# HGRN scores as needed 128x32 blocks with levels in pairs, and fp32 transposes as two 64-row tiles

## The chip, the cores and the metric

The kernel runs on one core of a Trainium2 chip. The metric is the device time of one execution in microseconds (us); the median of several runs is compared. In the profile PE is TensorE's matmuls, PEld its weight loads, DVE VectorE, ACT ScalarE, POOL GpSimd, SP the engine that issues most DMAs.

## The reference, cut to what matters

One layer for a prompt of 512 frames and a sample of 32: two branches, mLSTM (4 heads of 512) and HGRN2 (8 heads of 128), merged by sigmoid gates, then an output projection. The change concerns the HGRN2 branch, and wherever a tile is transposed.

```python
def _hgrn_chunk(S, inp):
    q, k, v, lf = inp
    g = jnp.cumsum(lf, axis=2)
    dec = jnp.exp(jnp.where(causal, g[:, :, :, None, :] - g[:, :, None, :, :], -jnp.inf))
    a = jnp.einsum('bhtc,bhtsc,bhsc->bhts', q, dec, k)
    o = jnp.einsum('bhtc,bhce->bhte', q * jnp.exp(g), S) + jnp.einsum('bhts,bhse->bhte', a, v)
    ...
```

The decay `dec` differs by channel, so the scores `a` are no plain product of q and k.

## The kernel before, in words

Activations stand transposed, channels on the 128 partitions and the 544 frames (32 of the sample, 512 of the prompt) in the columns. All dense products run in float32r, split into a high and a low part, three matmuls each; many projections are formed as pairs (`Two`) by a Strassen-like scheme, whose matmuls write the PSUM tiles named `d` (L608). TensorE's order is written by hand: a `Pump` holds the stream of `d` matmuls, six to a step, and the special work of a head is a generator (`mchain` for an mLSTM head, `chain` for an HGRN head) that yields the number of steps to run before its next piece. The order on VectorE and ScalarE comes from the framework's scheduler, by priorities and its own estimate of times. Small products use two PSUM tiles of two banks in turn (`paux`).

`chain(h)` computes an HGRN head. The scores of a block of 128 keys and 128 queries are made by levels: at level c = 1, 2, 4 ... 64, queries and keys that lie in neighbouring groups of c meet with the decay up to the border between them. At each level ScalarE copies the keys in a swapped order into `km` (L1818), TensorE multiplies them with the queries `qq`, for both blocks, 128x128 in fp32 (two passes each, L1832), VectorE copies what that level contributes into `at` by a mask (L1857), and multiplies the decay of the level into `kk` and `qq`, which lie in one tile `hkq` (L1850). Level 16 also makes the sample's scores out of copies (`snap`) that were taken at the four levels before (L1823, L1834, L1836, L1861). So of each 128x128 product only the blocks next to the diagonal at that level are used.

The rest of a head: `pd` transposes q times k for the diagonal (L1871), `ht` turns values and keys (L1902, L1903), `su` makes the states (L1921), `ho` the outputs from the triangles `aa` of `at`, which POOL cuts (L1797, L1945 to L1949); VectorE normalises them (L1951 to L1967), and `finish` of the head before, inside the next head's chain, turns them back (`hoT`, L1975, L1976) and multiplies by gain and gate (L1979, L1980). In `mchain`, `kt`, `kts`, `vt`, `vts` turn keys and values of an mLSTM head (L1122, L1135, L1157, L1175), and `yt` its outputs (L1307, L1308). All of these transposes are fp32 matmuls of 128 rows against the identity; a transpose is one pass.

Of the kernel before, what the change touches and what calls it, by code (L numbers as in the profile page):

```python
# [9 lines left out]
F32 = mybir.dt.float32  # L10
# [7 lines left out]
P = 128  # L18
# [18 lines left out]
QUADS = P // NS  # L37
STEPS = (2, 3, 3, 3, 3, 3, 3)
# [29 lines left out]
def hybrid_step(ctx: ExitStack, tc: tile.TileContext, a, o):  # L68
# [45 lines left out]
    def psplit(src, name, ring):  # L114
        hi, lo = pair_tile(name, ring)
        S.copy(hi, src)
        V.tensor_tensor(lo, src, hi.bitcast(F32), ALU.subtract)
        return hi, lo

# [196 lines left out]
    def masks():  # L316

        t = cp.tile([P, T], F32, tag="lm", name="lmask")
        u, n = t[:, :T].bitcast(U8), len(LEVELS) * HB
        return u[:, :n].rearrange("p (l t) -> p l t", l=len(LEVELS)), u[:, n : n + NS]  # L320
# [791 lines left out]
    def mchain(h, pump):  # L1112
# [5 lines left out]
        for b in range(NB):  # L1118
            yield 4 if h else 1
            pt = paux(f"kt{h}{b}")  # L1120
            for f in range(KH):
                PE.transpose(pt[:, 0, f * P : (f + 1) * P], kf[f][:, NS + b * P : NS + (b + 1) * P], ident)  # L1122
            kh, kl = slot(f"kwh{h}{b}", F32R), slot(f"kwl{h}{b}", F32R)
            wc = col[:, 10 + b, h : h + 1]
            with tc.high_priority():
                kh_ = S.mul(kh[:, :HD], pt[:, 0, :], wc)
                kl_ = V.scalar_tensor_tensor(kl[:, :HD], pt[:, 0, :], wc, kh[:, :HD].bitcast(F32), ALU.mult, ALU.subtract)
# [4 lines left out]
        yield 4 if h else 2  # L1132
        pt = paux(f"kts{h}")
        for f in range(KH):
            PE.transpose(pt[: 3 * NS, 0, f * P : (f + 1) * P], ksm[:, f], ident)  # L1135

        kws = small("kws", [3 * NS, HD], F32R, bufs=1)
        wc = cols[:, 1, h : h + 1]
        with tc.high_priority():
            S.mul(kws, pt[: 3 * NS, 0, :], wc)  # L1140
            lo = slice(2 * NS, 3 * NS)
            low = V.scalar_tensor_tensor(kws[lo], pt[lo, 0, :], wc[lo], kws[lo].bitcast(F32), ALU.mult, ALU.subtract)
# [6 lines left out]
        else:  # L1149
            yield max(0, max(pump.when["v", f] for f in range(KH)) - pump.done)  # L1150
            vt = t["vt"]
            vv = []
            for b in range(NB):
                yield 1
                pt = paux(f"vt{h}{b}")
                for f in range(KH):
                    PE.transpose(pt[:, 0, f * P : (f + 1) * P], vt[f][:, NS + b * P : NS + (b + 1) * P], ident)  # L1157
# [5 lines left out]
                with tc.high_priority():  # L1163
                    S.copy(vh[:, :HD], pt[:, 0, :])
                    V.tensor_tensor(vl[:, :HD], pt[:, 0, :], vh[:, :HD].bitcast(F32), ALU.subtract)
# [3 lines left out]
            yield 1  # L1169
            pt = paux(f"vts{h}")  # L1170
            vsm, copied = triple(vt, "vsm", t["copied"])
            with tc.issue_after(filled.ins):
                make_late(3 if h < MH - 1 else 2, copied)
            for f in range(KH):
                PE.transpose(pt[: 3 * NS, 0, f * P : (f + 1) * P], vsm[:, f], ident)  # L1175
            vs = small("vs", [3 * NS, VW], F32R, bufs=1)
            with tc.high_priority():
                S.copy(vs[:, :HD], pt[: 3 * NS, 0, :])
            G.tensor_copy(vs[:, HD:VW], vone)
            lo = slice(NS, 2 * NS)  # L1180
            with tc.high_priority():
                low = V.tensor_tensor(vs[lo, :HD], pt[lo, 0, :], vs[lo, :HD].bitcast(F32), ALU.subtract)
# [116 lines left out]
        for f in range(KH):  # L1299
# [3 lines left out]
            yield max(GAP - (16 if h == MH - 1 else 0 if h else 4) if f == 0 else 1 if h else 2, pump.when["z", f] - pump.done)  # L1303
            ft = h * KH + f
            pt = paux(f"yt{ft}")
            for b in range(NB):
                PE.transpose(pt[:, 0, b * P : (b + 1) * P], yb[b][:, f * P : (f + 1) * P], ident)  # L1307
            PE.transpose(pt[:, 1, :P], yb[NB][:, f * P : (f + 1) * P], ident)  # L1308
# [4 lines left out]
            with tc.high_priority():  # L1313
                V.scalar_tensor_tensor(c[:, NS:T], pt[:, 0, :], g, c[:, NS:T], ALU.mult, ALU.add)
                V.scalar_tensor_tensor(c[:, :NS], pt[:, 1, :NS], g, c[:, :NS], ALU.mult, ALU.add)
            with nullcontext() if 0 < h < MH - 1 else tc.high_priority():
# [978 lines left out]
```

## Time and profile before

| | |
|---|---|
| median of 3 runs | 1103.38 us (1103.07 to 1103.73) |
| span of the profiled execution | 1101.5 us, from the first to the last instruction |
| around the span, to the median of the runs | 1.9 us |
| mean granted TensorE clock | 0.998 |
| busy: PE, DVE, ACT, POOL | 99%, 84%, 63%, 19% |
| the eight HGRN heads | 627 to 862 us of the span |

A row of a group reads: line, engine, operation, out<-in, partitions x elements, count | busy us, mean ns of one | idle of the engine before them and what ended it. Of a matmul, 128*32 are rows and columns of the weight tile. A row of a timeline reads: start, length, instruction, count. Of two rows that overlap on PE, the distance of the starts is what the first one costs.

### The profile page before, as it was taken

The page shows a single profiled execution, that of the slowest core. Times are in us where ns is not written, and L with a number is a line of the kernel's source. Part 1 is how long each engine was busy: PE and PEld are TensorE (multiplying, and loading weights), DVE is VectorE, ACT ScalarE, POOL GpSimd, SP SyncE. Part 2 cuts the span into 40 slices and gives each one's busy share as a digit, 9 for nine tenths or more (in the row PEclk, how much of TensorE's full clock was granted, in tenths as well). Part 3 has the DMA queues.
Part 4 walks back from the last instruction along what each step waited for, and adds up shares of the span by engine and source line. Part 5 has one row for each costly group of instructions (what it writes and reads, how often), then busy time and mean ns, then how long its engine had stood idle before and what let it go on. Part 6 is the DMA issues. An engine that isn't in the chain of part 4 may idle for free.

```text
span 1101.5 us, 23773 instructions
## 1 busy us (share of the span) xinstructions
PE 1092.4 (99%) x8625; PEld 1070.9 (97%) x8625; DVE 922.8 (84%) x2103; ACT 693.1 (63%) x1579; POOL 209.5 (19%) x375
## 2 busy tenths in 40 slices
PE   9999999999999999999999999999999999999997
PEld 9899999999999999999999999999999999999997
DVE  7889988686896786986888799999999977778885
ACT  7777557754666554665656476776776666446683
POOL 5204010303022021202120123232232210000002
PEclk9999999999999999999999999999999999999999
DMA  7135415639355276554798665666765683337753
GB/s 241 50 124 157 156 58 185 158 125 220 119 178 179 93 178 176 164 167 146 212 261 254 172 145 141 144 135 152 159 145 150 155 222 103 110 90 242 247 180 121
DMA packets 97262, 176.58 MB, mean 160 GB/s; under 512 B 11284, under 2 KB 18580, under 8 KB 96888
## 3 DMA queue, kind: packets, MB, share of 16 engines
q1 hardware_dynamic: 81072, 141.01, 39.9%
q0 software_dynamic: 15184, 32.93, 16.2%
q8 instruction: 68, 1.11, 0.4%
q10 hardware_dynamic: 888, 1.12, 0.3%
q14 instruction: 50, 0.41, 0.1%
HBM read 150.10 MB, written 41.69 MB: 174 GB/s over the span
## 4 chain that ended last, share of the span: by engine, by line
PE 93%; DMA 3%; DVE 2%; issue 1%; SPq 0%; ACT 0%; POOL 0%; ACTq 0%; POOLq 0%
PE d L608 44%; PE ya L167 9%; PE yb L167 4%; PE q L167 4%; PE k L167 4%; PE C L1077 4%; PE nm L1257 3%; PE sc L1037 2%; PE pl L1832 2%; PE u L291 2%; PE d L460 2%; PE vp L1576 2%; DMA ws<-in_w_in 1%; PE ple L167 1%; PE kt L1122 1%; PE ht L1902 1%
## 5 line engine op out<-in xcount | busy, mean ns | idle before, releaser
L495 POOL DMA_DIRECT2D ws<-in_w_in x46 | 40.2, 875 | 211.3 <-DVE hkq L1850 32.2
L622 ACT COPY t<-d 128x272 f32<-128x272 f32 x153 | 58.0, 379 | 14.0 <-PE d L608 14.0
L1850 DVE TENSOR_TENSOR hkq<-hkq,q 128x288 f32<-128x288 f32 (+1 forms) x96 | 40.7, 431 | 2.6 <-PE pl L1834 1.0
L785 DVE SCALAR_TENSOR_TENSOR cv<-ub,vec,cv 128x547 f32<-128x547 f32 x48 | 37.6, 784 | 1.6 <-ACT cv L780 1.2
L1832 PE MATMUL pl<-hkq,km 128*128 128x128 f32 x224 | 36.2, 283 | 0.6 <-ACT km L1818 0.5
L1818 ACT COPY km<-hkq 128x256 f32<-128x256 f32 x56 | 23.9, 428 | 14.2 <-DVE hkq L1850 5.2
L1832 PEld LDWEIGHTS pl<-hkq,km 128*128 128x128 f32 x224 | 30.3, 189 | 2.0 <-ACT km L1818 1.5
L1191 DVE SCALAR_TENSOR_TENSOR c<-c,wi,Cs 128x258 f32<-128x258 f32 x32 | 15.3, 479 | 18.8 <-PE Cs L1189 18.5
L1354 DVE TENSOR_TENSOR y<-ya,y 128x272 f32<-128x272 f32 x48 | 18.9, 435 | 12.1 <-PE ya L167 10.3
L1089 ACT COPY Co<-C 128x258 f32<-128x258 f32 x30 | 9.8, 378 | 27.3 <-PE C L1077 24.9
L1857 DVE COPY_PREDICATED at<-lmask,pl 128x256 f32<-128x256 uint8 (+1 forms) x56 | 25.2, 451 | 0.1
L777 POOL COPY uo<-ub 128x3 f32<-128x3 f32 x16 | 18.7, 1167 | 34.5 <-DVE ub L631 26.6
L1268 ACT COPY y<-nm 128x516 f32<-128x516 f32 x16 | 9.4, 590 | 23.0 <-PE nm L1257 22.5
L133 POOL TENSOR_TENSOR wple50l<-wple5r,wple50h 128x256 fp32r<-128x256 f32 x1 | 0.7, 736 | 120.9 <-ACT wple50h L132 120.9
L961 POOL COPY ksm<-kf 128x96 f32<-128x96 f32 x16 | 7.1, 445 | 84.9 <-ACT kf L975 84.9
L961 POOL COPY vsm<-vt 128x96 f32<-128x96 f32 x12 | 6.3, 525 | 85.9 <-ACT vt L633 43.5
L1797 POOL TENSOR_SCALAR_AFFINE_SELECT aa<-at 128x128 f32<-128x128 f32 x32 | 19.6, 643 | 8.2 <-DVE at L1857 8.0
L581 POOL DMA_DIRECT2D ws<-in_w_in x14 | 14.6, 1043 | 33.1 <-DVE ws272l L133 27.3
L1245 DVE BATCH_NORM_STATS2 bs<-y 128x6 f32<-128x512 f32 (+1 forms) x20 | 13.8, 692 | 8.3 <-ACT y L1268 8.0
L1257 PE MATMUL nm<-vhl,sh 128*128 128x258 f32 x112 | 18.4, 286 | 0.0
L376 POOL DMA_DIRECT2D w_pg_d<-in_w_pg x16 | 13.1, 818 | 25.1 <-issue 21.4
L1956 ACT ACTIVATE osq<-kq 128x128 f32<-128x128 f32 x32 | 9.8, 305 | 12.4 <-DVE kq L1951 12.1
(4735 smaller groups left out, 5086.7 us busy)
## 6 DMA issues: line engine op xcount, KB each, us to landing
ws<-in_w_in POOLq DMA_DIRECT2D x60, 256.0 KB, 4.9
ws<-in_w_in SPq DMA_DIRECT2D x46, 256.0 KB, 3.9
ya_d<-y SPq DMA_DIRECT2D x32, 272.0 KB, 2.3
y<-ya_d SPq DMA_DIRECT2D x24, 272.0 KB, 3.3
w_out_d<-in_w_out POOLq DMA_DIRECT2D x24, 256.0 KB, 6.5
w_pg_d<-in_w_pg POOLq DMA_DIRECT2D x24, 256.0 KB, 6.5
c<-in_C SPq DMA_DIRECT2D x16, 258.0 KB, 3.8
out_Cs<-c SPq DMA_DIRECT2D x16, 258.0 KB, 3.8
```

The costliest lines, as they stand in the source:

```text
L167: PE.matmul(both[b][:m, :TH], part(w, off + k * step, m, x), xx[:, half(b)], start=(k == 0 and j == 0), stop=(k == n - 1 and j == 2),)
L291: PE.matmul(both[b][:m, :TH], part(w, off + k * step, m, x), xx[:, half(b)], start=(k == 0 and j == 0), stop=(k == KD - 1 and j == 2),)
L495: G.dma_start(t, piece(u, i), accum_op=ALU.add)
L608: PE.matmul(ps, ww[:, c], xx, start=(start and k == 0 and j == 0), stop=end, skip_group_check=not start,)
L622: self.kept = S.copy(t, ps)
L785: V.scalar_tensor_tensor(cv[:, :547], ub[:, j : j + 547], vcol(V_CW + 4 * ft + j), cv[:, :547], ALU.mult, ALU.add)
L1077: PE.matmul(pn[g][:, :VH], kw[b][x][:, f * P : (f + 1) * P], vv[b][y][:, g * VH : (g + 1) * VH], start=(b == 0 and j == 0), stop=(b == NB ...
L1257: PE.matmul(pn[:, g, :VH], st[j][x][:, (i - j) * P : (i - j + 1) * P], vv[j][y][:, g * VH : (g + 1) * VH], start=(j == 0 and q == 0), stop ...
L1818: low = S.copy(km.rearrange("p (n j c) -> p n j c", j=2, c=c), view(kk, HB, ((2 * c, NA // (2 * c)), (c - HB, 2), (1, c))),)
L1832: PE.matmul(out, km[:, b * P : (b + 1) * P], view(qq, b * P, dims), start=True, stop=True)
L1850: V.tensor_tensor(x, x, d, ALU.mult)
L1857: V.copy_predicated(at[:, :n], lmask[:, li, :n], pn[:, 0, :n])
```

## The change

It has three parts.

1. The scores are made only where they are used: for each quarter of 32 keys a matmul of 128x32 weights and 32 queries (64 at level 64), whose output goes to the 32 PSUM partitions of that quarter, so that four stand side by side in the array (`scores`). The levels go in pairs (1), (2, 4), (8, 16), (32, 64): of a pair's first level the queries are kept as a copy `oldq` (and the sample's pair `olds`) and the keys in one half of `kms`, and both levels are multiplied at the second. The sample is made with each level below 32 (four equal tiles). `collect` puts the results into a strip `near` of 96 columns by mask, into `far` (level 32) or straight into `at` (level 64), and four copies spread the strips into `at`. The tile `oldq` lies in has the old name `lmask`.
2. A transpose of 128 rows becomes two of 64 rows (`turn`), whose outputs go to two PSUM banks, and all readers of the PSUM tile take them apart by `turned` and `quarters`. Of the sample only the 64 rows that hold it are turned.
3. Two groups of transposes stand back to back, where a group stood alone: `kt` in pairs, `kts` with `vt0`, `vt1` with `vt2`, `vt3` with `vts`, `yt` in pairs, both `ht`, and `hoT` with `pd`, which is moved from level 1 (and `hoT` from behind level 16) to ahead of level 16's block. The gain of the head is multiplied into the gate ahead of time.

```diff
+    def turn(pt, i, src, eye=None):
+        n = src.shape[-1]
+        for r in range(2):
+            k = slice(r * HP, (r + 1) * HP)
+            at_ = ident[k, k] if eye is None else eye[k, P - (r + 1) * HP : P - r * HP]
+            PE.transpose(pt[:n, r, i * HP : (i + 1) * HP], src[k], at_)
...
         for b in range(NB):
-            yield 4 if h else 1
-            pt = paux(f"kt{h}{b}")
-            for f in range(KH):
-                PE.transpose(pt[:, 0, f * P : (f + 1) * P], kf[f][:, NS + b * P : NS + (b + 1) * P], ident)
+            if b % 2 == 0:
+                yield 8 if h else 2
+                pts = [paux(f"kt{h}{b + i}") for i in range(2)]
+                for i in range(2):
+                    for f in range(KH):
+                        turn(pts[i], f, kf[f][:, NS + (b + i) * P : NS + (b + i + 1) * P])
...
+        def scores(pn, i, c, km, snap):
+            for b in range(2):
+                for g in range(QUADS):
+                    key, w = b * P + g * NS, max(c, NS)
+                    out = pn[g * NS : (g + 1) * NS, i, b * w : (b + 1) * w]
...
+                    PE.matmul(out, km[:, key : key + NS], ask, start=True, stop=True)
+            if c < NS:
+                for g in range(QUADS):
+                    PE.matmul(
+                        pn[g * NS : (g + 1) * NS, i, 2 * NS : 3 * NS],
+                        olds[:, 0] if snap else kk[:, csmp],
+                        olds[:, 1] if snap else qq[:, csmp],
+                        start=True,
+                        stop=True,
+                    )
+
+        def collect(ps, li, c):
+            if c < NS:
+                V.copy_predicated(near, lmask[:, li], ps[:, : 3 * NS])
+            elif c == NS:
+                S.copy(far, ps[:, : 2 * NS])
+            else:
+                for g in range(2):
...
+        def turn_both():
+            if h:
+                pt = turn_out(h - 1)
+            pn = paux(f"pd{h}")
+            for b, c_ in enumerate([c_ for c_, _, _ in chunks] + [slice(NA, NA + P)]):
+                turn(pn, b, kq[:, c_])
+            with tc.high_priority():
+                V.tensor_reduce(dg, turned(pn, NB + 1), AX.XY, ALU.add)
+            if h:
+                finish(h - 1, pt)
+
         for li, c in enumerate(LEVELS):
...
+                if first_:
+                    S.copy(
+                        oldq.rearrange("p (n j c) -> p n j c", j=2, c=c),
+                        view(qq, 0, ((2 * c, NA // (2 * c)), (HB + c, 2), (1, c))),
+                    )
+                    if c < NS:
+                        S.copy(olds, hs[h]["pair"][:, :, csmp])
                 low = S.copy(
                     km.rearrange("p (n j c) -> p n j c", j=2, c=c),
                     view(kk, HB, ((2 * c, NA // (2 * c)), (c - HB, 2), (1, c))),
                 )
-                if li < QUADS:
-                    S.copy(snap[:, :, li], hs[h]["pair"][:, :, csmp])
             held.append(low)
-            yield STEPS[li]
...
+            if not first_:
+                n = STEPS[li] + (STEPS[li - 1] if li else 0)
+                if li == 4:
+                    yield n // 2
+                    turn_both()
+                    n -= n // 2
+                yield n
+
+                pn = paux(f"pl{h}{c}")
+                if li:
+                    scores(pn, 0, c // 2, kms[:, 0], True)
+                scores(pn, 1, c, km, False)
...
-                V.copy_predicated(at[:, :n], lmask[:, li, :n], pn[:, 0, :n])
-                if smp:
-                    for i in range(QUADS):
-                        d = slice(i * NS, (i + 1) * NS)
-                        V.copy_predicated(at[d, NA:HB], smask[d], pn[d, 1, d])
+                if not first_:
+                    if li:
+                        collect(pn[:, 0], li - 1, c // 2)
+                    collect(pn[:, 1], li, c)
+            if c == 2 * NS:
+                for g in range(QUADS):
...
+                    S.copy(at[k, :NA].rearrange("p (b q s t) -> p b q s t", b=2, q=2, s=2)[:, :, g // 2], both_)
```

TensorE, head 3, before: around the scores of level 16 (`pl316`); `hkq3` holds queries and keys, `d...` are the dense matmuls between.

```order
L608 MATMUL d521_10311<-xl5_892,ws452h_10542 128x272
L608 MATMUL d521_10311<-xh5_891,ws452l_10543 128x272
L1832 MATMUL pl316_10642<-hkq3_9838,km316_10610 128x128 x2
L1834 MATMUL pl316_10642<-hkq3_9838 128x32
L1836 MATMUL pl316_10642<-snap_10431 128x128
L608 MATMUL d521_10311<-xh6_908,ws452h_10542 128x272
```

The same place after; `lmask_2805` is `oldq` and `olds`, the queries of level 8.

```order
L625 MATMUL d520_10756<-xfl3_1327,wa2252h_10958 128x272
L625 MATMUL d520_10756<-xfh3_1326,wa2252l_10959 128x272
L1891 MATMUL pl316_11112<-lmask_2805,km38_11007 32x32 x8
L1894 MATMUL pl316_11112<-lmask_2805 32x32 x4
L1891 MATMUL pl316_11112<-hkq3_10210,km38_11007 32x32 x8
L1894 MATMUL pl316_11112<-hkq3_10210 32x32 x4
L625 MATMUL d521_10757<-xh4_886,ws452h_11015 128x272
```

Levels 8 and 16 have become one block of 24 small matmuls, with 18 dense ones ahead of it, and 18 more between the transposes and the pair before.

TensorE, head 3, after: `hoT2` (outputs of head 2) and `pd3`, between the blocks `pl34` and `pl316`.

```order
L625 MATMUL d761_11020<-xh5_891,wa1276l_10941 128x272
L129 MATMUL hoT2_11059<-anti_123,kq2_9663 128x64 x4
L129 MATMUL hoT2_11059<-ident_104,kq2_9663 128x64 x4
L2084 MATMUL hoT2_11059<-anti_123,osb_10696 128x64
L129 MATMUL pd3_11069<-ident_104,kq3_10211 128x64 x10
L625 MATMUL d761_11020<-xh6_908,wa1276h_10940 128x272
```

Before, `pd3` stood six dense matmuls behind level 1 and `hoT2` six behind level 16, each alone; both are now one block.

VectorE, head 3, before: the scaling of head 2's outputs (`kq2`, `osb`), on which `hoT2` waits.

```order
L1850 TENSOR_TENSOR hkq3_9838<-hkq3_9838,q03_10188 128x2x16x8
L185 SCALAR_TENSOR_TENSOR hr_10406<-rsq_u_10415,hr_10406 128x5
L133 TENSOR_TENSOR ws276l_10586<-ws176_10337,ws276h_10585 128x512
L1961 TENSOR_TENSOR kq2_9365<-kq2_9365,hr_10406 128x512
L1967 TENSOR_SCALAR osb_10288<-osb_10288,hr_10406 128x128
L133 TENSOR_TENSOR ws376l_10633<-ws376_10340,ws376h_10632 128x512
L1850 TENSOR_TENSOR hkq3_9838<-hkq3_9838,q03_10188 128x2x9x16
```

And after.

```order
L1904 COPY_PREDICATED at3_10866<-lmask_2805,pl34_10977 128x96
L202 SCALAR_TENSOR_TENSOR hr_10830<-rsq_u_10839,hr_10830 128x5
L200 TENSOR_TENSOR rsq_u_10839<-hr_10830 128x5
L201 SCALAR_TENSOR_TENSOR rsq_u_10839<-rsq_u_10839,hv_10829 128x5
L202 SCALAR_TENSOR_TENSOR hr_10830<-rsq_u_10839,hr_10830 128x5
L2070 TENSOR_TENSOR kq2_9663<-kq2_9663,hr_10830 128x512
L1970 TENSOR_TENSOR hkq3_10210<-hkq3_10210,q03_10619 128x2x18x8
L2076 TENSOR_SCALAR osb_10696<-osb_10696,hr_10830 128x128
L1970 TENSOR_TENSOR hkq3_10210<-hkq3_10210,q03_10619 128x2x16x8
```

The scaling now stands between the masked copy of level 4 and the update of level 8; before it stood behind the update of level 8.

265 lines of the change are left out of this document (155 added, 110 removed).

## The prediction

> **What bounds the kernel.** I read the engines' shares and the chain that ended last, then the stretch of the eight HGRN heads by windows, then the groups of the instructions that the change replaces.
>
> ```profile
> PE 1092.4 (99%) x8625; PEld 1070.9 (97%) x8625; DVE 922.8 (84%) x2103; ACT 693.1 (63%) x1579; POOL 209.5 (19%) x375
> PE 93%; DMA 3%; DVE 2%; issue 1%; SPq 0%; ACT 0%; POOL 0%; ACTq 0%; POOLq 0%
> 627.00:862.00 235.00, 234.36 (x1901) 231.68 (x1899) 227.66 (x631) 167.48 (x464) 65.59 (x94) 1.00 0.64 147
> L1832 PE MATMUL pl<-hkq,km 128*128 128x128 f32 x224 | 36.2, 283 | 0.6 <-ACT km L1818 0.5
> L1871 PE MATMUL pd<-ident,kq 128*128 128x128 f32 x40 | 5.7, 272 | 0.0
> L1122 PE MATMUL kt<-ident,kf 128*128 128x128 f32 x64 | 9.7, 274 | 0.0
> L1307 PE MATMUL yt<-ident,y 128*128 128x128 f32 x64 | 10.0, 273 | 0.2 <-DVE y L1296 0.2
> ```
>
> TensorE carries 93% of the chain, at a clock of 1.00 in the stretch. Its matmuls there wait 0.6 us for `km` and for next to nothing else, so a microsecond taken from TensorE is one from the time, as long as nothing else becomes late. In the heads' stretch VectorE is nearly full too (227.66 of 235), ScalarE is not (167.48). The `x224` are records of passes: an fp32 matmul has two, 112 matmuls being 224; a transpose has one.
>
> A record's length (0.28 us) overlaps the next; what an instruction costs is the distance of starts. So I price a block from the start of the dense matmul before it to that of the second dense matmul behind it, less two dense paces.
>
> ```profile
> 627.62 0.29 PE L608 MATMUL d<-xh,ws472l 128*128 128x272 f32 x1
> 627.75 0.64 PE L1832 MATMUL pl<-hkq,km 128*128 128x128 f32 x4
> 628.13 0.38 PE L608 MATMUL d<-xfh,ws249h 128*128 128x272 f32 x1
> 628.35 0.29 PE L608 MATMUL d<-xfl,ws249h 128*128 128x272 f32 x1
> 628.47 0.29 PE L608 MATMUL d<-xfh,ws249l 128*128 128x272 f32 x1
> 628.85 0.29 PE L608 MATMUL d<-xfh,ws249l 128*128 128x272 f32 x1
> 628.98 0.71 PE L1871 MATMUL pd<-ident,kq 128*128 128x128 f32 x5
> 629.65 0.29 PE L608 MATMUL d<-xfl,ws249h 128*128 128x272 f32 x1
> 670.59 0.29 PE L608 MATMUL d<-xh,ws450l 128*128 128x272 f32 x1
> 670.72 0.61 PE L1832 MATMUL pl<-hkq,km 128*128 128x128 f32 x4
> 671.31 0.47 PE L1836 MATMUL pl<-snap 128*128 128x128 f32 x2
> 671.74 0.29 PE L608 MATMUL d<-xl,ws450h 128*128 128x272 f32 x1
> ```
>
> The dense pace is 0.125 us (628.35 to 628.47, and from 628.47 three more to 628.85). A level of scores costs 628.35 - 627.62 - 0.25 = 0.48 us; level 16, with the sample's extra products, 671.74 - 670.59 - 0.25 = 0.90. A head has six of the one and one of the other, 3.78 us; eight heads 30.2. Five transposes cost 629.65 - 628.85 - 0.25 = 0.55, 0.11 each. The change retiles 380 of them (by the program's order kt 64, kts 16, vt 48, vts 12, yt 80, pd 40, ht 80, hoT 40): 41.8 us. So 72 us of TensorE are in play.
>
> **Scores in 128x32 tiles.** The kernel already has such tiles once, in the sample's values:
>
> ```profile
> 46.56 0.63 PE L1576 MATMUL vp<-wv3h,x 128*128 128x512 f32 x2
> 47.03 0.40 PE L1576 MATMUL vp<-wv3l,x 128*128 128x512 f32 x1
> 47.36 0.62 PE L1586 MATMUL vq<-wv0r,xg 128*32 128x512 f32 x1
> 47.38 0.62 PE L1586 MATMUL vq<-wv3r,xg 128*32 128x512 f32 x1
> 47.81 0.59 PE L1586 MATMUL vq<-wv0r,xg 128*32 128x512 f32 x1
> 47.83 0.59 PE L1586 MATMUL vq<-wv3r,xg 128*32 128x512 f32 x1
> 48.35 0.72 PE L1576 MATMUL vp<-wv4h,x 128*128 128x512 f32 x2
> 48.91 0.40 PE L1576 MATMUL vp<-wv4l,x 128*128 128x512 f32 x1
> ```
>
> Four tiles start within 0.02 us and run side by side; the second pass follows 0.45 later, of which 0.03 is the first weight load (0.62 against 0.59): 0.42 for 512 columns, 0.83 ns each. The dense pace is 0.235 (46.56 to 47.03 is two), so the block costs 48.91 - 47.03 - 3 x 0.235 = 1.18, and entering and leaving the tiling 1.18 - 2 x 0.42 = 0.34.
>
> After the change a level below 32 has three rounds of four tiles (two blocks of keys, one of the sample) of 32 columns in two passes: six passes in a row per tile; level 32 four, level 64 four of 64 columns. That is 34 short passes and 4 long ones a head. A short pass takes at least its load, 0.03, its columns being 0.027. At most it takes the issue of four loads and four matmuls: four starts in 0.02 are 7 ns each, eight are 0.055. I take 0.04, nearer to the streamed row, and for a long pass 0.065, between its columns (0.053) and 0.08: 1.62 us a head (1.24 to 2.2). Levels in pairs give four tilings a head instead of eight or seven.
>
> The Trainium skill, "TensorEngine Tiling (Array Packing)", Instruction Overhead, says that a matmul of one column lasts as long as one of 60, and warns against taking the tiling from a dimension that is already small; no run here shows it for tiles. By it a short pass would be 60 x 0.83 = 0.05 us, an estimate, and the scores would save 2.7 us less than I sum.
>
> **Transposes as two 64-row tiles.** No two row tiles run in the trace. The nearest are transposes of 4-row tiles, which all stand in one row group:
>
> ```profile
> 90.73 0.42 PE L167 MATMUL q<-cs3h,wq001l 128*128 128x272 f32 x2
> 91.08 1.27 PE L916 MATMUL cols<-ident,row 4*128 4x4 f32 x18
> 92.22 0.28 PE L918 MATMUL cols<-ident,r 4*96 4x4 f32 x3
> 92.43 0.52 PE L167 MATMUL q<-cs0h,wq010h 128*128 128x272 f32 x2
> 92.78 0.29 PE L167 MATMUL q<-cs0l,wq010h 128*128 128x272 f32 x1
> ```
>
> They move four columns only and still take (92.22 - 91.08) / 18 = 0.063 us: that is the weight load of 128 columns; with 96 columns 0.05. The second dense matmul started at 90.86, so the block costs 92.78 - 90.86 - 3 x 0.125 = 1.55, and entering and leaving 1.55 - 18 x 0.063 - 3 x 0.05 = 0.27. I take 0.30 for each change of tiling, between this and 0.34.
>
> A transpose becomes two loads of 128 columns and two matmuls of 64 columns (0.053 each). If the two row tiles work side by side, the pair is bound by one load, 0.063; by the columns alone it would be 0.053; if the loads go one after the other, 0.126, more than the 0.11 of now. I take 0.063, as the column tiles did run side by side. The order has 46 blocks of them (four of these are splinters of `yt12`, cut by dense matmuls): 380 x 0.063 + 46 x 0.30 = 37.7 us against 41.8. So it saves 4.1 us; 2.2 with 0.34 a change, 9.2 with 0.053 and 0.27. The change of tiling eats most of it: a block of eight saves 0.88 - 0.50 - 0.30 = 0.08 us, the lone `kts0` loses 0.11.
>
> The scores: 8 x (1.62 + 4 x 0.30) = 22.6 against 30.2, 7.6 saved; with the ends 1.8 to 11.6.
>
> **The other engines.** These rows tell what is taken from VectorE and how the one chain that is pulled forward stands:
>
> ```profile
> L1857 DVE COPY_PREDICATED at<-lmask,pl 128x256 f32<-128x256 uint8 x48 | 21.4, 446 | 0.1
> L1861 DVE COPY_PREDICATED at<-lmask,pl 32x32 f32<-32x32 uint8 x32 | 6.0, 189 | 0.3
> L1818 ACT COPY km<-hkq 128x256 f32<-128x256 f32 x55 | 23.4, 426 | 14.2 <-DVE hkq L1850 5.2 <-DVE hr L185 3.4 <-DVE rsq_u L184 2.0
> 655.92 0.39 PE L1949 MATMUL ho<-s,hkq 128*128 128x128 f32 x2
> 669.83 0.69 DVE L133 TENSOR_TENSOR ws274l<-ws,ws274h 128x512 fp32r<-128x512 f32 x1
> 670.43 0.68 DVE L1961 TENSOR_TENSOR kq<-kq,hr 128x512 f32<-128x512 f32 x1
> 671.03 0.28 DVE L1967 TENSOR_SCALAR osb<-osb,hr 128x128 f32<-128x128 f32 x1
> 672.36 0.38 PE L1975 MATMUL hoT<-anti,kq 128*128 128x128 f32 x2
> ```
>
> Masked copies fall from 56 of 256 or 288 columns and 32 small ones (48 x 0.446 + 8 x about 0.48 + 6.0 = 31) to 40 of 96 columns, about 0.26 each between 0.19 and 0.446: 21 us less VectorE in the stretch that is full. The rest there is small: `finish` in three products instead of two, 1 us over eight heads. ScalarE gets, a head, three copies of `oldq` (0.43 each, as `km`), two of `olds` in place of four of `snap`, and seven for the far blocks of `at`: about 2.8 us, 22 in all, 190 of some 225; filled, not the bound. POOL loses two copies and a larger memset a head; the DMAs stay as they are, but for one smaller table. In the mLSTM part `yt` is read in two halves by row, 16 more short VectorE instructions, under an engine with a fifth of its time free. These I cost at nothing; the pairs cover them, since 36 dense matmuls (4.5 us) now stand ahead of a pair where 18 stood ahead of a level.
>
> What is not free is `hoT`. Its inputs were scaled 671.31 - 656.31 = 15.0 us behind the end of `ho`, and `hoT` came 1 us behind that. Now it stands 78 dense matmuls and two blocks of scores behind `ho`: 9.75 + 0.54 + 0.78 = 11.1 us. In the new order VectorE has 35 instructions from the sum of `ho` to this scaling, which, each by its group's length less 0.08 (669.83 to 670.43 is 0.60 at a length of 0.69), make 10.4 us, with a masked copy among them that waits for level 4's block; from there to the scaling are about 2.1 to 2.7 us, and TensorE gets there in 18 dense matmuls, 2.25. So a wait of 0 to 0.5 us a head; with the same for level 16, which needs `hoT`'s PSUM read out within 2.25 us, I put 0.25 a head, 2 us (0 to 4).
>
> **The sum.** 7.6 + 4.1 - 2.0 = 9.7 us from the profiled span of 1101.5: 1091.8. The median of the runs, 1103.38, is 1.9 above the span, so 1093.7; I say 1094. With the ends: 11.6 + 9.2 - 0 = 20.8 gives 1083; 1.8 + 2.2 - 4 = 0 gives no change.
>
> **Rivals.** *The row tiles' weight loads go one after the other* (slower): 356 transposes then have two loads and 24 one: 736 x 0.063 + 13.8 = 60.2, a loss of 18.4 in place of a gain of 4.1: 1103.4 - 7.6 + 18.4 + 2 = 1116. It decides from 0.088 us a pair on, where 5.6 us, the scores' gain less the waits, are used up. For it: all loads in the trace that follow each other on one row group are serial at 0.063. Against it: the column tiles' loads overlap. The Trainium skill, "TensorE: Matmul & The Clock Gate", Part 3, states 3.07 times for four row tiles, against this rival; no run here shows it.
>
> *The issue of so many small matmuls sets the pace* (slower): a head has 152 passes; if each took 0.027, its columns with no tile beside it, they would be 4.1 us and with the tilings 5.3 a head against 3.78: 12.2 lost, 1103.4 + 12.2 - 4.1 + 2 = 1114. It decides from 0.019 a pass on. For it: 24 matmuls in a block, where the trace shows four; against it 7 ns between starts.
>
> *The waits grow* (no change): 1.5 us a head at `hoT`, level 16 or `su` (whose transposes now end 12 dense matmuls ahead of it for both operands) are 12 us, as much as is saved: 1103.4. For it: VectorE full and 15 us shortened to 11. Against: 21 us less of its work.
>
> *Tilings change cheaply*: at 0.2 instead of 0.30, 78 changes give 7.8 more: 1086. Only that the two rows differ by 0.07 speaks for it.
>
> **Chances.** Forecast 0.56 (own range 1088 to 1101), cheap changes 0.11, waits 0.14, serial loads 0.11, issue 0.08. About 0.2%, 2.2 us, is what a measurement can tell from no change. Faster: 0.56 + 0.11 and 0.01 of the waits, 0.68; same: most of the waits, 0.12; slower: the rest, 0.20. The range leaves out most of the two slow rivals: 1084 to 1109.
>
> **What would show it.** Right: blocks of eight `kt` at about 0.8 us, of twelve tiles at 0.55 and 24 at 0.8; TensorE still at 99%; VectorE in the heads' stretch about 205 us of 220. Wrong: starts of `turn` pairs 0.12 apart (serial loads); blocks of 24 at over 1.3 us (issue); idle time of TensorE named VectorE or ScalarE at `hoT`, `pl` or `su` above 4 us (waits).

## The result, and the profile after

The changed kernel is 0.6% slower: 1110.88 us median (1108.42 to 1112.16) against 1103.56 (1103.07 to 1104.73) of the kernel before beside it, a ratio of 1.0061, 95% interval [1.0047, 1.0074]. Forecast were 1094. Its profiled execution took 1108.42 us, the shortest of the four; its span is 1106.7, 5.2 more than before.

The engines' shares and the chain of the page, and the heads' stretch by windows (PE, PEld, DVE, ACT, POOL busy us and instructions, granted clock, DMA share, GB/s):

```profile
PE 1086.5 (98%) x9941; PEld 1045.3 (94%) x9941; DVE 912.3 (82%) x2079; ACT 710.7 (64%) x1643; POOL 191.5 (17%) x367
PE 82%; DVE 8%; ACT 6%; issue 2%; DMA 1%; DVEq 0%; ACTq 0%
627.00:862.00 235.00, 228.27 (x2963) 212.84 (x2962) 215.69 (x588) 181.92 (x516) 53.30 (x84) 1.00 0.64 144
```

TensorE has less to do, 1086.5 us busy in the whole execution against 1092.4, but it is idle more: 6.7 of the 235 us of the stretch, against 0.6 before. And the chain now runs through VectorE and ScalarE for 14% of the span, against 2% before. The work went away, and waits came. The waits of PE (what for; us in total, times, longest):

```profile
PE hoT L129 <- DVE kq L2070: 3.4, 7, 0.8
PE su L2030 <- ACT hkq L2019: 2.4, 7, 0.4
PE d L625 <- DVE ws48l L150: 1.8, 1, 1.8
PE d L625 <- DVE ws412l L150: 1.8, 1, 1.8
...
PE yt L129 <- DVE c L1377: 0.9, 2, 0.4
PE kt L129 <- DVE kwl L1147: 0.7, 2, 0.5
```

This view has 13.3 us in all; before, it had 1.8 us, in three waits that came once each. TensorE's blocks themselves, from its timeline: a pair of levels, and both `ht` with the `su` behind them.

```profile
704.34 0.29 PE L625 MATMUL d<-xfh,wa2251l 128*128 128x272 f32 x1
704.56 0.33 PE L1891 MATMUL pl<-lmask,km 128*32 128x32 f32 x16
...
705.12 0.39 PE L625 MATMUL d<-xh,ws451h 128*128 128x272 f32 x1
705.35 0.28 PE L625 MATMUL d<-xl,ws451h 128*128 128x272 f32 x1
```

```profile
681.14 0.29 PE L625 MATMUL d<-xfh,ws374l 128*128 128x272 f32 x1
681.36 0.53 PE L129 MATMUL ht<-ident,hi 64*128 64x64 f32 x10
681.73 0.52 PE L129 MATMUL ht<-ident,hkq 64*128 64x64 f32 x10
682.17 0.39 PE L625 MATMUL d<-xh,wa1151h 128*128 128x272 f32 x1
682.40 0.28 PE L625 MATMUL d<-xl,wa1151h 128*128 128x272 f32 x1
...
684.66 1.16 PE L2030 MATMUL su<-hi,hkq 128*128 128x128 f32 x8 [0.35 <-ACT hkq L2019]
```

The pair costs 705.35 - 704.34 - 0.25 = 0.76 us (forecast 0.78). Ten transposes cost 682.40 - 681.14 - 0.25 = 1.01, where ten whole ones cost 1.09. Added up over all such blocks of the two timelines, the scores take 21.9 us, against 30.0 at the typical costs of before, and the transposes without their waits 39.8 against 42.8: some 11 us saved on TensorE. The time that came back, by the same way of counting: 5.2 us at `hoT` with `pd`, 4.6 at `su`, 3.6 at the two `d` in the mLSTM part, 1.9 at other `d` in the HGRN heads, 1 each at `yt` and `kt`, 1 at `ho` and `ht`: 18 in all, so 7 to be lost, and TensorE's last matmul starts 5.9 us later (1100.53 against 1094.67). A microsecond is left unassigned.

### The profile page after: what moved, and what is told of

The parts are those of the page before. It is cut to its first block, busy times and chain, and to the rows that moved or that the text cites. A ratio compares the mean times of both kernels' runs of the same rounds, so it can differ in the third digit from the quotient of the medians.

```text
span 1106.7 us, 26357 instructions
## 1 busy us (share of the span) xinstructions
PE 1086.5 (98%) x9941; PEld 1045.3 (94%) x9941; DVE 912.3 (82%) x2079; ACT 710.7 (64%) x1643; POOL 191.5 (17%) x367
## 4 chain that ended last, share of the span: by engine, by line
PE 82%; DVE 8%; ACT 6%; issue 2%; DMA 1%; DVEq 0%; ACTq 0%
PE d L625 36%; PE ya L184 9%; PE yb L184 4%; PE q L184 4%; PE k L184 4%; PE C L1094 4%; PE nm L1312 3%; PE sc L1054 2%; PE u L308 2%; PE d L477 2%; PE vp L1634 2%; DVE hkq L1970 1%; PE ple L184 1%; PE su L2030 1%; ACT km L1940 1%
## 5 line engine op out<-in xcount | busy, mean ns | idle before, releaser
L794 POOL COPY uo<-ub 128x3 f32<-128x3 f32 x16 | 10.1, 628 | 43.5 <-DVE ub L648 28.5
L393 POOL DMA_DIRECT2D w_out_d<-in_w_out x16 | 13.5, 974 | 18.4 <-issue 16.3
L1855 POOL TENSOR_SCALAR_AFFINE_SELECT aa<-at 128x128 f32<-128x128 f32 x32 | 15.3, 780 | 6.0 <-ACT at L1990 6.0
L1312 PEld LDWEIGHTS nm<-vhl,sh 128*128 128x128 f32 x112 | 15.4, 190 | 0.5 <-ACT Co L1106 0.5
L1023 DVE TENSOR_TENSOR ql<-q,qh 128x272 fp32r<-128x272 f32 x24 | 9.4, 433 | 7.4 <-ACT qh L1022 6.4
L1068 ACT CAST sh<-dm 128x512 fp32r<-128x512 f32 (+3 forms) x16 | 7.2, 457 | 12.9 <-DVE dm L1062 12.9
```

Source lines behind the costliest of these rows:

```text
L393: G.dma_start(late[g][n][k], src, accum_op=ALU.add)
L1312: PE.matmul(pn[:, g, :VH], st[j][x][:, (i - j) * P : (i - j + 1) * P], vv[j][y][:, g * VH : (g + 1) * VH], start=(j == 0 and q == 0), stop ...
```

## Experiments

"Scores alone" means the changed scores with every transpose as one of 128 rows, where it stood before. Times are medians; the kernel before ran beside each group at 1105.0, 1104.5, 1103.8, 1104.7 and 1104.6 us.

| kernel | us | ratio to before, 95% interval |
|---|---|---|
| e1 scores alone | 1107.7 | 1.0025 [1.0016, 1.0034] |
| e2 changed, whole transposes | 1112.9 | 1.0079 [1.0065, 1.0092] |
| e3 scores, 64-row tiles, each group alone | 1118.6 | 1.0124 [1.0108, 1.014] |
| e4 changed, `ht` apart | 1112.1 | 1.0062 [1.0047, 1.0078] |
| e5 scores alone, spread on POOL | 1103.5 | 0.999 [0.9981, 0.9999] |
| e6 scores alone, no collecting copy on ScalarE | 1103.2 | 0.9985 [0.9974, 0.9995] |
| e7 scores alone, levels single | 1099.0 | 0.995 [0.9935, 0.9965] |
| e8 changed, no collecting copy on ScalarE | 1110.0 | 1.0053 [1.0036, 1.007] |
| e9 scores alone, pairs (2,4), (8,16) | 1109.9 | 1.0059 [1.0044, 1.0073] |
| e10 scores alone, pair (32,64) | 1101.1 | 0.9973 [0.9963, 0.9982] |
| e11 scores alone, pair (2,4) | 1097.7 | 0.9944 [0.9932, 0.9956] |
| e12 changed, levels single | 1139.7 | 1.0327 [1.0314, 1.0341] |
| e13 e11 with the mLSTM transposes changed | 1105.1 | 1.0008 [0.9998, 1.0018] |
| e14 e11 with `ht` changed | 1096.5 | 0.9933 [0.9919, 0.9947] |
| e15 e11 with `hoT` and `pd` moved | 1131.0 | 1.0236 [1.022, 1.0253] |
| e16 e11, spread on POOL | 1098.2 | 0.9946 [0.9933, 0.9959] |
| e17 e14, `ht` of 128 rows | 1097.9 | 0.9944 [0.9928, 0.9959] |
| e18 changed, `hoT` and `pd` back in place | 1112.8 | 1.0076 [1.0063, 1.0089] |

**e1, e2, e3, e4: which part.** The first theory was that the scores pay as forecast and that the grouped and moved transposes make the waits.

```diff
 e1, e2:  def turn(pt, i, src, eye=None):
-        for r in range(2):
-            ... PE.transpose(pt[:n, r, i * HP : (i + 1) * HP], src[k], at_)
+        PE.transpose(flat[:n, i * P : (i + 1) * P], src, ident if eye is None else eye)
 e1, e3:  each group alone again, pd behind level 1, hoT behind level 16
 e4:
-        yield 2
-        pts = [turn_head(src) for src in (ii, kk)]
-        keep(pts[0], it, its); keep(pts[1], kt, kts); diagonal()
+        yield 0
+        keep(turn_head(ii), it, its); diagonal()
+        yield 2
+        keep(turn_head(kk), kt, kts)
```

> Only the scores are changed (128x32 tiles, levels in pairs); every transpose is one of 128 rows again and stands where it stood before. Theory (the scores' tiles pay as forecast, the loss comes from the waits that the grouped and moved transposes make): the blocks of scores save 8.1 us, as they did in the changed kernel, and no wait is added but a little where VectorE now collects two levels at once: 1095 to 1097 us, a ratio of 0.993. Rival (the scores' extra copies on ScalarE and their later collection make the waits): idle time of TensorE at su and pl of some 5 us stays, and the time is 1100 to 1104.

> The changed kernel with its groups and its order, but each transpose is one of 128 rows, so no change of tiling at a transpose. Theory (grouping and moving make the waits): the waits at su and hoT stay (7 us), only the net gain of the 64-row tiles, 1.5 us, is lost: 1109 to 1113 us. Rival (the tilings of 64 rows cost more than they show in their own blocks): the time falls to that of the scores alone, 1095 to 1098.

> The changed scores and transposes as two 64-row tiles, but each group alone and where it stood before. Theory: 0.067 us a pair and 0.30 a change of tiling, with 83 groups: 380 x 0.067 + 83 x 0.30 = 50.4 us against 41.8, so 8.6 lost beside the 8.1 that the scores save, no new waits: 1103 to 1106 us. Rival (the tilings themselves cost more than their blocks show): above 1112.

> The changed kernel, but the two transposes of a head's values and keys (ht) stand two steps apart as before, so that ScalarE has copied the values when the keys are turned. Theory: the wait of su, 4.6 us over eight heads, goes, and eight changes of tiling come back, 2.4: 1107 to 1109.5 us. Rival (su waits for ScalarE's queue, filled by the scores' copies, not for the pair of transposes): su still waits some 4 us, and the time is 1112 to 1114.

The theory fell at once. e1 has none of the transposes' changes and still loses 2.7 us. Its windows row and its waits:

```profile
627.00:862.00 235.00, 223.92 (x2794) 212.76 (x2793) 208.45 (x576) 182.58 (x515) 52.64 (x84) 1.00 0.63 143
```

```profile
PE su L2088 <- ACT hkq L2062: 3.3, 6, 0.5
PE ht L132 <- ACT kit L2063: 2.8, 5, 1.3
PE d L635 <- DVE ws288l L160: 1.4, 1, 1.4
...
PE d L635 <- DVE ws277l L160: 0.5, 1, 0.5
```

TensorE is idle 11.1 us of the stretch, against 0.6 before. (The last row is one of six alike, a head each.) Between e1 and e2, the grouped and moved transposes, whole, cost 5.2 us. Between e2 and the changed kernel (1112.9, 1110.9) the 64-row tiles seem to save 2.1, but the two intervals overlap. With each group alone (e3) the tiles lose 10.9 over e1, near the 8.6 worked out from 0.067 a pair and 0.30 a change of tiling; `su` waits 7.3 us there, 3.3 in e1. (e3 lies in its rival's range, above 1112, because e1 is itself some 12 us above what the theory put it at.) e4 missed: the wait of `su` went, but `hoT` waited 6.8 us in place of 3.4, 3.3 of it in one wait of the profiled execution, the slowest of its four, and no time was gained. In part the lateness of `su` showed at another place.

**e5, e6, e7, e8: who is late.** The chain of e1 at the end of a head shows it. ScalarE's timeline, then `ht` and `su` on TensorE:

```profile
710.37 0.21 ACT L1934 COPY at<-pl 128x64 f32<-128x64 f32 x1
710.48 0.26 ACT L1938 COPY at<-pl 64x128 f32<-64x128 f32 x1
710.63 0.58 ACT L2062 COPY hi<-ht 128x512 f32<-128x512 f32 x1
711.11 0.25 ACT L2063 COPY kit<-ht 32x128 f32<-32x128 f32 x1
711.38 0.26 ACT L1938 COPY at<-pl 64x128 f32<-64x128 f32 x1
711.66 1.22 ACT L2024 COPY at<-at 32x128 f32<-32x128 f32 x4
...
713.62 0.56 ACT L2062 COPY hkq<-ht 128x512 f32<-128x512 f32 x1
```

```profile
711.41 0.77 PE L132 MATMUL ht<-ident,hkq 128*128 128x128 f32 x5 [0.25 <-ACT kit L2063]
714.24 1.16 PE L2088 MATMUL su<-hi,hkq 128*128 128x128 f32 x8 [0.54 <-ACT hkq L2062]
```

The pair of levels 32 and 64 delivers all far blocks at once, so seven small copies (L1934, L1938, L2024; 2 us) stand in ScalarE's queue among the copies of `ht`, for which `su` waits. The engine is idle a fifth of the stretch, and still too late here. Two theories: A, these copies; B, the pairing of the levels.

```diff
 e5 (e1), e6 (e1), e8 (changed):   spreading
-                    S.copy(at[k, :NA]..., both_)
+                    G.tensor_copy(at[k, :NA]..., both_)
 e6, e8:   levels 32 and 64
-                S.copy(far, ps[:, : 2 * NS])
+                V.tensor_copy(far, ps[:, : 2 * NS])
                 ... and so for the two copies of level 64
 e7 (e1):
-            first_ = li % 2 == 1
+            first_ = False        # seven blocks of one level each
```

> The kernel with the scores alone changed (1107.7 us), but the four copies that spread the strips into at are made by POOL instead of ScalarE. Theory A (ScalarE's seven small copies at the end of a head's levels, 2.0 us, stand in its queue ahead of the copies of ht, so ht and su wait, 1.2 us a head): with 1.2 us of the 2.0 gone the wait at su goes, half of that at ht stays: 8 x 0.8 = 6 us less, 1101 to 1104. Rival B (the waits come from VectorE's order, where two levels are collected at once, and ht waits for that): the waits at ht and su stay, 1106 to 1109.

> The same kernel, with the four spreading copies on POOL and the three copies from PSUM (levels 32 and 64) on VectorE, so ScalarE has none of the seven. Theory A: neither ht nor su waits any longer; the wait of d for VectorE's split, 0.6 us a head, stays or grows by 0.2: 1107.7 - 9.4 + 1 = 1098 to 1101. Rival B: 1106 to 1109, VectorE being the later one.

> The kernel with the scores alone changed, but the levels one by one: seven blocks of tiles a head instead of four, no kept queries (oldq, olds). Three more changes of tiling a head cost 3 x 0.30 x 8 = 7.2 us by the measured blocks. Theory A (ScalarE's copies at the end): ScalarE loses three copies of 0.43 and two of 0.25 a head, but not the seven at the end; ht and su still wait, and the wait of d for VectorE's split goes (0.6 a head), since VectorE collects one level at a time: 1107.7 + 7.2 - 4.8 = 1108 to 1112. Rival B (pairing of the levels makes all the waits): 1107.7 + 7.2 - 13 = 1100 to 1104.

> The changed kernel (1110.9 us), with the four spreading copies on POOL and the three copies from PSUM on VectorE. Theory A: su no longer waits for ScalarE's copies of ht (0.6 us a head), hoT still waits for VectorE (0.6 a head) and the mLSTM part keeps its 3.2 us: 1110.9 - 4.8 = 1105 to 1108. Rival B: 1110 to 1113.

e5 as theory A: 4.2 us less. Beside the row below, `ht` waits 0.8 us in place of 2.8, and the waits for `ws27..l` stay.

```profile
PE su L2088 <- ACT hkq L2062: 1.2, 6, 0.2
```

e6 gained only 0.4 more, not 4: `su` no longer waits, but the six waits for `ws27..l` grow to 0.5 to 0.8, and `ht` waits once 1.2 us for `at` from VectorE and once 1.7 for ScalarE. e8 gained 0.9 only, within the noise; `hoT` still waits. e7 beat both expectations: although its scores take 28.3 us by blocks, 6.4 more than in e1, it is 8.7 us faster than e1, so in e1 the pairs cost some 15 us of waiting. Its waits on PE, all of them, its heads' stretch, and its spreading copies in the same head:

```profile
PE warm L1489 <- DVE emc L1316: 1.1, 1, 1.1
PE yt L132 <- DVE y L1373: 0.2, 1, 0.2
```

```profile
627.00:862.00 235.00, 234.15 (x2887) 222.48 (x2886) 216.99 (x591) 182.30 (x496) 58.84 (x89) 1.00 0.64 147
```

```profile
705.59 1.22 ACT L2024 COPY at<-at 32x128 f32<-32x128 f32 x4
```

With level 32 in a block of its own, the spreading is done before level 64 is multiplied (its `pl` starts at 707.81), out of the way of `ht`. So B holds, and A is a part of it: the last pair makes the copies late. But moving the copies alone (e5, e6) gave back 4.2 to 4.5 us, under a third of the 15; e7 also ends VectorE's late splits, 4.4 us of waits of `d` in e1. ScalarE is as busy in the stretch as in e1 (182.3 against 182.6 us).

**e9, e10, e11: which pair.**

```diff
 (e1)
-            first_ = li % 2 == 1
+            first_, second = li in KEPT, li - 1 in KEPT    # e9: (1, 3)  e10: (5,)  e11: (1,)
```

> Scores alone changed, transposes as before; the levels (2, 4) and (8, 16) in pairs, 1, 32 and 64 single, so a pair costs 0.75 us of TensorE where two blocks cost 1.04. Theory C (the pair of levels 32 and 64 moves five of ScalarE's copies behind the last block of scores, and that makes ht and su late): those waits are gone; the pair (8, 16) keeps the wait of d for VectorE's split, 0.6 us a head, since VectorE waits for that block with the split behind it: 1099.0 - 8 x 0.58 + 8 x 0.6 = 1099 to 1100. Rival D (every pair makes waits at ht and su): 1102 to 1105.

> The same with only the levels 32 and 64 in a pair. Theory C: the waits at ht and su are back, 1.2 us a head, against 0.35 a head that the pair saves: 1099.0 + 8 x 0.85 = 1104 to 1107, and no wait of d for a split. Rival D or B (all pairs together make it): 1099 to 1101.

> The same with only the levels 2 and 4 in a pair. Theory C: no wait at ht or su, none of d, 0.29 us a head saved: 1099.0 - 2.3 = 1096 to 1098. Rival D: above 1099.

e10 costs 2 us over e7, less than expected: `su` costs 1.63 us at the median where e7 has 1.17 and e1 1.93, and `ht` hardly waits, so the full 1.2 us a head needs the other pairs as well. e11 as expected. e9 missed by 10 us, and as it differs from e11 in nothing but the pair (8, 16), it prices that pair where 32 and 64 are single: 12.1 us. There `d` waits for VectorE's splits as in e1, and a wait of 7.5 us in nine places appeared that was not on the list, `pl` for `km`. One of them, with the issue of a weight piece's DMA on POOL's queue, ScalarE, and TensorE:

```profile
831.35 0.86 POOL L609 DMA_DIRECT2D ws<-in_w_in  x1 [3.93 <-DVE ws279l L161]
834.01 1.22 ACT L2025 COPY at<-at 32x128 f32<-32x128 f32 x4
836.43 0.62 ACT L160 CAST ws479h<-ws 128x512 fp32r<-128x512 f32 x1 [1.20 <-DMA ws<-in_w_in]
837.40 0.43 PE L1920 MATMUL pl<-hkq,km 128*32 128x64 f32 x16 [1.43 <-ACT km L1975]
```

The four copies stand in ScalarE's queue ahead of level 64's `km`, but so does the cast of a weight piece, and here the cast sets the time: ScalarE is idle 1.20 us behind the copies until the piece lands, and only then casts it and copies `km` (836.95). The DMA was issued only when VectorE had split the piece before it, `ws279l`, the same split that `d` waits for. VectorE does this split behind the block of the pair (8, 16). In seven of the nine places ScalarE was idle ahead of such a cast, 0.24 to 3.60 us. So a late VectorE reached TensorE by two ways, its own split and a DMA issued late. In the last six of these heads ScalarE waits 0.03 us or less at these casts in e7, and in e11 up to 0.77 in three of them. (In the kernel before it waits there too, 0.94 to 1.11 us a head, and `pl` does not wait for it; that the late split and the copies together used up this room is a reading, not shown by a run of its own.) Why the single levels make e9 slower than e1, which has the same pair (8, 16), was not taken further apart.

**e12, e13, e14, e15: the transposes' parts.** e12 is the changed kernel with e7's single levels; e13, e14 and e15 put one part each on e11.

```diff
 e12 (changed):   first_ = False
 e13 (e11):  kt, kts, vt, vts, yt by turn(...) in 64-row tiles, grouped as in the changed kernel
 e14 (e11):  both ht by turn(...), back to back
 e15 (e11):  hoT and pd, 128 rows
+                if li == 4:
+                    yield n // 2
+                    turn_both()
+                    n -= n // 2
```

> The changed kernel with all its transposes (64-row tiles, groups back to back, moved), but the levels of the scores one by one. Theory C: what is left above the 1099.0 us of the same scores with plain transposes is the price of the transposes' part: 3.2 us in the mLSTM heads, in the HGRN heads the wait of hoT for VectorE's scaling (0.6 a head); su waits less, as ScalarE's copies come earlier: 1103 to 1107. Rival (the transposes' part is harmless once the pairs are gone): 1097 to 1100.

> The scores in tiles with only the levels 2 and 4 in a pair (1097.7 us), and the transposes of the mLSTM heads alone changed (kt, kts, vt, vts, yt as two 64-row tiles, groups back to back); those of the HGRN heads as before. Theory: the blocks gain nothing (a block of eight saves 0.04 us), and the waits of the changed kernel's mLSTM part (d for VectorE's split behind the yt pairs, 1.8 us twice, yt and kt for VectorE) come with it: + 3.2 us, 1100 to 1102.5. Rival (the mLSTM part is neutral; the loss there came from elsewhere): 1096.5 to 1098.5.

> The same scores, and of the transposes only ht changed (64-row tiles, values and keys back to back). Theory: the two blocks of 0.55 become one of 1.0, 0.1 us a head saved, and su waits for ScalarE, which copies both products only after the pair: up to 0.6 a head, as in the changed kernel: 1097.7 + 0 to 4 = 1098 to 1102. Rival (no wait once levels 32 and 64 are single, because ScalarE is free there): 1096 to 1098.

> The same scores, and of the transposes only the move: hoT and pd stand together ahead of level 16's block, as transposes of 128 rows. Theory (TensorE reaches hoT some 12 us behind ho, VectorE scales its inputs 15 us behind ho): a wait of 2 to 4.5 us a head, so 1097.7 + 7 x 3 = 1112 to 1130. Rival (the long wait with single levels came from the 64-row tiles or from ht): 1097 to 1101.

e12 missed by over 30 us; e15 shows why, as its theory said: it is the move of `hoT`, which waits 20.6 us in e12 and 17.7 in e15. From the timelines, VectorE has scaled the inputs of `hoT` 14.0 us behind the end of `ho` in the kernel before and 13.9 in e7, 15 in e15, but 11.4 in the changed kernel and 10.9 in e1, both with all levels in pairs. TensorE reaches the moved `hoT` 11.1 us behind `ho` in the changed kernel, 0.4 us too early, and 12.4 in e15, 2.7 too early. But e15 loses 4.7 to 5.7 us in most heads for waits of at most 2.8. One wait and what follows, first the wait, then the windows with the granted clock third from the end:

```profile
706.13 0.66 PE L133 MATMUL hoT<-anti,kq 128*128 128x128 f32 x2 [2.70 <-DVE kq L2129]
```

```profile
700.00:704.00 4.00, 3.43 (x48) 3.01 (x46) 3.77 (x14) 2.04 (x5) 0.00 (x0) 1.00 0.73 219
...
707.00:708.00 1.00, 1.00 (x7) 1.00 (x6) 0.53 (x1) 0.00 (x0) 0.00 (x0) 0.50 1.03 158
...
710.00:711.00 1.00, 1.00 (x6) 0.90 (x4) 0.00 (x0) 0.00 (x0) 0.00 (x0) 0.50 0.49 129
...
712.00:713.00 1.00, 1.00 (x9) 1.00 (x9) 1.00 (x4) 0.95 (x3) 0.73 (x1) 0.99 0.00 0
```

After this wait TensorE runs 6 us at half its clock, so a wait of 2.7 us costs about 5.7. Two of the six long waits of e15 have a stretch of 6.8 us at 0.50, and four one of 3.4, which makes such a wait 4.4. The Trainium skill, "TensorE: Matmul & The Clock Gate", Part 1, tells of such a gate: half rate after an idle window of about 3.4 us, full again after a busy one. The trace agrees with the half rate and with steps of 3.4 us, but shows the half rate after 2.7 us of idle time.

e13 loses 7.4 us, twice the expected: 3.7 by the end of the mLSTM part, as in the changed kernel, and then one wait of 2.5 us for `km` in the first heads with 3.4 us at a clock of 0.50 behind it. That wait is again a cast that stood ahead of `km` and had to wait 2.08 us for its DMA; whether the changed transposes made it late is open. The cause in the mLSTM part is visible in the changed kernel, on VectorE and then TensorE:

```profile
303.34 1.99 DVE L1383 TENSOR_TENSOR c<-c,z 128x544 f32<-128x544 f32 x3
305.24 0.72 DVE L107 TENSOR_TENSOR hm4l<-c,hm4h 128x544 fp32r<-128x544 f32 x1
305.88 0.72 DVE L1383 TENSOR_TENSOR c<-c,z 128x544 f32<-128x544 f32 x1
306.51 0.72 DVE L107 TENSOR_TENSOR hm5l<-c,hm5h 128x544 fp32r<-128x544 f32 x1
307.15 0.68 DVE L150 TENSOR_TENSOR ws48l<-ws,ws48h 128x512 fp32r<-128x512 f32 x1
```

```profile
307.89 0.39 PE L625 MATMUL d<-xh,ws48l 128*128 128x272 f32 x1 [1.75 <-DVE ws48l L150]
```

With both pairs of `yt` read, VectorE gates four tiles and splits two in one run, and the split of a weight piece stands behind it, which TensorE needs at 306.14 and gets at 307.83. It is the grouping that does this: the waits for `ws48l` and `ws412l` are there with grouped whole transposes too (e2, 1.2 us each) and absent with 64-row tiles one group at a time (e3); with both they are 1.8.

e14 has the lowest median, though not clear of e11: no wait above 0.2 us but the one at the start, and both `ht` in one block save 0.13 us a head.

**e16, e17, e18.**

```diff
 e16 (e11):   G.tensor_copy in place of S.copy for the spreading
 e17 (e14):   ht as transposes of 128 rows, still back to back
 e18 (changed):   hoT and pd apart and where they stood before, still 64-row tiles
```

> The same scores, all transposes as before, and the four copies that spread the strips made by POOL instead of ScalarE. Theory: ScalarE loses 1.2 us a head, the waits of pl for km (2.1 us) and the 0.05 a head at su go: 1095 to 1097. Rival (POOL cuts the triangles later and ho waits for them): 1098 to 1101.

> As the fastest so far (scores in tiles, only levels 2 and 4 in a pair, both ht back to back; 1096.5 us), but ht as transposes of 128 rows. Theory (the 64-row tiles pay only where twenty stand in one block: 0.97 against 2 x 0.55): 8 x 0.13 = 1 us more and no wait, 1097 to 1098.5. Rival (putting ht together is what gained, the tiles nothing): 1096 to 1097.

> The changed kernel (1110.9 us) with only one thing undone: hoT and pd stand apart again and where they stood before, still as 64-row tiles. Theory (the move made hoT's wait): the wait of 0.6 to 0.7 us a head goes, 4.9, eight changes of tiling come back, 2.4, so 1108 to 1109.5. Rival (VectorE's lateness only shows elsewhere, as when ht was set apart): the wait reappears at d for VectorE's splits or at su, 1111 to 1114.

e16 is no better than e11, and `ho` does not wait as its rival said: `pl` still waits 1.6 us for `km`, now behind casts that wait 1.45 and 2.51 us for their DMA, with no copy of the strips ahead of them. So with these levels single the four copies were not what mainly held `km` up. e17 is 1.4 us behind e14; the tiles may pay in that one block, but the runs overlap (1096.4 to 1099.0; 1096.8 to 1101.6). e18 went as its rival said: `su` waits 4.4 us for ScalarE, `d` for VectorE's splits. It also shows the half clock once more. The same wait for `ws48l`, 1.8 us, stands in the changed kernel and in e18, and of the window from 310 to 311 us, some 2 us behind it, the first has this row and the second that:

```profile
310.00:311.00 1.00, 1.00 (x11) 1.00 (x10) 1.00 (x2) 0.14 (x1) 0.95 (x1) 1.00 0.46 162
```

```profile
310.00:311.00 1.00, 1.00 (x7) 1.00 (x6) 0.44 (x1) 0.03 (x1) 0.00 (x0) 0.50 0.67 203
```

So a wait of 1.8 us is followed by some 3 us at half the clock in one execution and not in another. That may be why the changed kernel's other runs are 1.7 to 3.7 us above the profiled one: a stretch of 3.4 us at half the clock costs 1.7, and the two slowest, 3.2 and 3.7 us above, have mean granted clocks of 0.997 and 0.996 against 0.999. The third has 0.999, and none of the three was profiled, so it stays open.

## Why the prediction was wrong

The forecast's direction failed, not its TensorE arithmetic.

- **Scores**: 8.1 us saved by the typical blocks, 7.6 forecast. The blocks cost 0.54 and 0.76 (0.54 and 0.78 forecast), single ones 0.52. The rivals of serial loads and of the issue fell: pairs of `turn` cost 0.067 us, blocks of 24 0.76 and not 1.3. By the Trainium skill, "TensorEngine Tiling (Array Packing)", Instruction Overhead, a matmul of few columns lasts as long as one of 60; at the 0.83 ns a column of the trace before that makes a pair's block 0.9 us, an estimate from that page; the trace shows 0.76.
- **Transposes**: forecast were 0.063 us a pair and 0.30 a change of tiling; 0.067 and 0.30 fit the blocks (0.84 us for eight pairs of `kt`, 0.97 to 1.02 for ten of `ht`). The saving is about 3.0 us in blocks, against 4.1; in time e2 shows 2.1, not clear of the noise.
- **"These I cost at nothing; the pairs cover them, since 36 dense matmuls (4.5 us) now stand ahead of a pair where 18 stood ahead of a level"**: this is the step that failed. A pair has twice the time ahead of it, but it hands VectorE and ScalarE the work of two levels at once, and what TensorE wants next stands behind that work. With the scores alone the pairs cost some 15 us of waiting (e1 against e7), more than the scores save; of them the pair (8, 16) is the dearest, 12.1 us where 32 and 64 are single (e9 against e11).
- **"Filled, not the bound", ScalarE's 22 us**: a part of the same step. The work was hidden on average (182 of 235 us busy) and not where it stood: seven copies in a row among `ht`'s copies, on the only path to `su`. e5 gave back 4.2 us by moving four of them to POOL.
- **VectorE's readers of `yt`, also at nothing**: in the mLSTM part an engine with a fifth of its time free was late by 1.8 us twice, because the grouping put its work in one run (e13: 3.7 us).
- **Waits, 2 us (0 to 4)**: of these only `hoT` was in the sum, and there the working was near: TensorE got to it 11.1 us behind `ho`, as counted, and waited 0.44 us a head, inside the 0 to 0.5; 3.4 in all, and 5.2 with what the block cost. `su`, the splits and the mLSTM part were left out of the sum. All of them are some 18 us. The sign that I named for it, more than 4 us at `hoT`, `pl` or `su`, is there: 3.4 and 2.4. The rival *the waits grow* named the mechanism and priced it at 1.5 us a head; with 12 us it gave no change, and its chance of 0.14 was far too low for a change that moved four groups on a chain through three engines.
- **21 us less VectorE work**: its masked copies did fall by 20.9 us, and it helped, but not enough: `hoT`'s inputs came 2.6 us earlier (11.4 against 14.0; the 15.0 that I read is the first head's), and `hoT` 3.7 (15.2 to 11.5).

## The faster version

e14 beats both kernels: 1096.5 us, 0.9933 [0.9919, 0.9947] of before. It keeps the 128x32 tiles, pairs only levels 2 and 4, turns both `ht` in 64-row tiles back to back, and leaves every other transpose as it was. By blocks its scores take 26.0 us, so 4.0 of the 8.1 are kept, and `ht` gives 1.0 more; TensorE's last matmul starts 5.8 us earlier than before. Its page and all its waits on PE:

```profile
PE 1086.2 (99%) x9665; PEld 1054.8 (96%) x9665; DVE 906.0 (83%) x2051; ACT 707.5 (65%) x1619; POOL 201.3 (18%) x367
```

```profile
PE warm L1490 <- DVE emc L1317: 1.1, 1, 1.1
PE yt L133 <- DVE y L1374: 0.2, 1, 0.2
PE u L319 <- ACT wf0h L160: 0.2, 1, 0.2
```

TensorE is busy as long as in the changed kernel (1086.2 and 1086.5 us): the 12 us between the two spans, 1094.7 and 1106.7, are waiting. (The medians differ by 14.4.)

## What to carry to other kernels

When small steps of an engine on the critical path are merged into larger ones, the engines behind it get their work in bursts: look at the queue of each at the burst, at what stands ahead of the one instruction that the critical engine wants next and what that waits for in its turn, a DMA for instance, and count an engine's share of busy time as no cover. Moving work earlier is safe only by the measured time at which its inputs are ready, and that time changes with everything else in the change. Try the parts apart, since here the half that pays was hidden by the half that does not.

## What had not been expected of the hardware

A wait of TensorE can cost more than its length. In the traces of all these kernels a granted clock of 0.50 followed each of the 15 waits of 2.3 to 3.3 us, 4 of the 14 waits of 1.75 to 1.97 us (once in e9 and e18, twice in e4), and none of the 27 waits between 1.0 and 1.7 us within the kernels; it lasted 3.4 us in most cases and 6.8 in four. What decides between the 4 and the 10 is open.

A single level's block of tiles, 24 passes, costs 0.52 us, more than the four whole passes of a level before (0.475), although it multiplies a quarter as much, and the sample. Most of it is the change of tiling: two single blocks cost 1.04 us and a pair's block 0.76, so one change less is worth 0.28.
